# Attention's stage of a diffusion layer in the program's order on four engines, with its steps at ticks and less adaLN work inside

## The chip, the core and the metric

The kernel runs on one core of a Trainium2 chip. The metric is the device time of one execution in microseconds; three executions of the kernel before have a median of 1446.35 us (1445.36 to 1450.94). The engines are named as in the profile: PE is TensorE, DVE is VectorE, ACT is ScalarE, POOL is GpSimd and SP is the queue that issues nearly all transfers.

## The reference: what is computed

One layer of a diffusion backbone: adaLN, two-dimensional neighbourhood attention, and a gated convolutional FFN. There are 256 latent tokens (four rows of 64) and 256 context tokens, a width of 2048, 16 heads of 128 and an FFN width of 5504, all in float32. Cut to its core:

```
sh1, sc1, g1, sh2, sc2, g2 = split(silu(c) @ w_ada + b_ada, 6)
h, hc = modulate(rms_norm(x), sh1, sc1), modulate(rms_norm(ctx), csh1, csc1)
q, k, v = split(h @ w_qkv, 3); qc, kc, vc = split(hc @ w_qkv, 3)    # q and k: rms_norm per head
p = softmax(concat(q @ k_window * scale + bias, q @ kc * scale))
x = x + g1 * ((p @ concat(v, vc)) @ w_o)
hf = modulate(rms_norm(x), sh2, sc2)
x = x + g2 * conv_ffn(hf)
```

## The kernel before

**Products.** Every weight is fetched in tiles of 256 rows by 512 columns (512 KB, buffer `wr`, four of them) and split into a high and a low part: ScalarE rounds the high part `wh` (L155, three buffers), VectorE subtracts to get the low part `wl` (L156, two buffers). The activations are split in the same way (`hh` and `hl`). A product is then three matmuls: high by high, high by low, low by high. The splits are written two tiles ahead of their use (`ahead`, `weight`).

**Projections.** `project(c0, nt)` makes 512 columns (four heads, called a group) of Q, K or V for `nt` token tiles of 128: four for K and V (latent and context), two for Q (latent only). For each of eight weight tiles and each token tile it issues six matmuls of 512 columns (L378 to L380), into the PSUM banks `pj`, four in all. The order is Q0, K1, Q1, V2, K2, Q2, K3, Q3, V3 (K0, V0 and V1 come from an earlier stage). This is attention's stage; in the profile it lies between 204 and 601 us.

**Attention beside it.** While the next group is projected, the four heads of the group before are worked on: for each head two score products with bias add, maximum, exponential, sum and scaling (`scores`), two transposes of the probabilities with a high and a low part (`turn`), and the product with V (`weigh`). These pieces stand in the list `side`, from which a piece is taken after token tiles (`side.tick`), with a fractional rate. Between two groups the list is emptied, and then all K and Q tiles of the coming group are normed and transposed (`norm_transpose`): four squares with sums on ScalarE (L521), a power on GpSimd (L195), two Newton steps and a scaling on VectorE (L196 to L200, L526), four transposes on TensorE (L532), a high part on ScalarE (L534) and a low part on VectorE (L535). This is the order as written; a scheduler then sets the order of every engine's instructions, with the scores at high priority.

**adaLN beside it.** Three of adaLN's six vectors (`g1T`, `sh2T`, `gs2T`) are made in this stage too: twelve columns of 512, each the sum of eight pieces. A piece loads 512 KB (`wa`, a ring of three buffers) and multiplies it by `silu(c)`, either on ScalarE with sums on GpSimd (L276, L277) or on VectorE alone (L274, L279). A finished column is totalled (L285, on VectorE), transposed on TensorE (L288) and reduced and biased (L291, L294, L296). There are 97 pieces, placed by `ada.tick(0.44 * nt)` per weight tile, so that all are used up by the end of the stage.

**w_o.** The output projection has five groups, WO0 to WO4. WO0 covers the twelve heads that are done; beside it the rest of group 3's heads is worked on (`rest`, one piece per `cn / 340` of a tick). The others follow, with a residual step into `x1` on VectorE (L779), squares on ScalarE and their sum (L788). WO4 has 256 columns and uses the `ms` banks. Then come the norm and the FFN (products at L727 and L733).

Of the kernel before, what the change touches and what calls it, by code (L numbers as in the profile page):

```python
# [15 lines left out]
P = 128  # L16
# [10 lines left out]
KT = 2  # L27

RATE, RATE3 = 0.46, 0.36
# [21 lines left out]
def block_kernel(  # L51
# [29 lines left out]
    turns = []  # L81
# [47 lines left out]
    rp = cp.tile([NH * NDR, 31], F32, name="rp")  # L129
    nc.scalar.dma_start(rp, rpb)  # L130
# [16 lines left out]
    def wpair(src, k0, kn, c0, cn):  # L147
# [4 lines left out]
        with ExitStack() as order:  # L152
            for ins in hold:
                order.enter_context(tc.issue_after(ins))
            a = nc.scalar.copy(hi[:, :kn, :cn], w[:, :kn, :cn])  # L155
            b = nc.vector.tensor_tensor(  # L156
                out=lo[:, :kn, :cn], in0=w[:, :kn, :cn], in1=hi[:, :kn, :cn].bitcast(F32),
                op=ALU.subtract,
            )
# [7 lines left out]
    for g, cols in ((0, (0,)), (1, (D, 0)), (2, (2 * D, D, 0)), (3, (D, 0, 2 * D))):  # L167
        for c in cols:
            plan.extend((w_qkv, kt, KT, c + g * CH, CH) for kt in range(0, KD, KT))
# [21 lines left out]

    def rsqrt_newton(pool, v, n, name, bufs=2):

        r, t = [pool.tile([P, n], F32, tag=name + i, name=name + i, bufs=bufs) for i in "rt"]
        nc.gpsimd.tensor_tensor(out=r, in0=v, in1=mhalf[:, :n], op=ALU.pow)  # L195
        nc.vector.tensor_mul(t, r, r)  # L196
        nc.vector.scalar_tensor_tensor(
            out=t, in0=t, scalar=-0.5, in1=v, op0=ALU.mult, op1=ALU.mult
        )
        nc.vector.scalar_tensor_tensor(  # L200
            out=r, in0=t, scalar=1.5, in1=r, op0=ALU.add, op1=ALU.mult
        )
        return r
# [48 lines left out]
    def ada_tasks(pool, i, c, dst, gcol=None):  # L252
# [10 lines left out]
        def part(q):  # L263
# [6 lines left out]
            for k in range(KT):  # L270
                s = sT[:, q * KT + k, 0:1]
                first = q < 2 and k == 0
                if first:
                    nc.vector.tensor_scalar_mul(acc, w[:, k, :], s)  # L274
                elif pool_:
                    nc.scalar.mul(w[:, k, :], w[:, k, :], s)  # L276
                    nc.gpsimd.tensor_add(acc, acc, w[:, k, :])  # L277
                else:
                    nc.vector.scalar_tensor_tensor(  # L279
                        out=acc, in0=w[:, k, :], scalar=s, in1=acc, op0=ALU.mult, op1=ALU.add  # L280
                    )

        def finish():
            acc = st["acc", 0]
            nc.vector.tensor_add(acc, acc, st["acc", 1])  # L285
            sp = ms()
            for b in range(4):
                nc.tensor.transpose(sp[:, b * P : (b + 1) * P], acc[:, b * P : (b + 1) * P], ident)  # L288
            d = dst[:, 4 * c : 4 * c + 4]
            bc = S_B + i * KD + 4 * c  # L290
            nc.vector.tensor_reduce(  # L291
                out=d, in_=sp.rearrange("p (b t) -> p b t", t=P), axis=AX.X, op=ALU.add
            )
            nc.vector.tensor_add(d, d, sm[:, bc : bc + 4])  # L294
            if gcol is not None:
                nc.vector.scalar_tensor_tensor(  # L296
                    out=d, in0=d, scalar=1.0, in1=sm[:, gcol + 4 * c : gcol + 4 * c + 4],
                    op0=ALU.add, op1=ALU.mult,
                )

        return [(lambda q=q: load(q), lambda q=q: part(q)) for q in range(KD // KT)], finish

    def ada_pieces(cols):
# [5 lines left out]
        def piece(i):  # L309
# [5 lines left out]
            if i % n == 1 and i > n:  # L315
                cols[i // n - 1][1]()
            with tc.issue_after(last[0]), tc.issue_after(last[1]):
                if i < len(parts):
                    parts[i]()
                else:  # L320
                    cols[-1][1]()
# [15 lines left out]
    xp = xctx.enter_context(tc.tile_pool(name="xp", bufs=1))  # L337
    s32 = xp.tile([P, KD, 32], F32, name="s32")
# [31 lines left out]
    def nat(psl, tt0, w, kt0, n, first, last):  # L370

        wh, wl = w
        for i, pt in enumerate(psl):
            ts = slice((tt0 + i) * P, (tt0 + i + 1) * P)
            for k in range(n):
                kt = kt0 + k
                a, z = first and k == 0, last and k == n - 1
                nc.tensor.matmul(pt, hh[:, kt, ts], wh[:, k, :], start=a, stop=False)  # L378
                nc.tensor.matmul(pt, hh[:, kt, ts], wl[:, k, :], start=False, stop=False)  # L379
                nc.tensor.matmul(pt, hl(kt, ts), wh[:, k, :], start=False, stop=z)  # L380
# [131 lines left out]
    def row2k(name):  # L512
        return ap.tile([P, CH], F32, tag="r2", name=name, bufs=3)

    def norm_transpose(pt, gcol, dh, dl, t0):

        ss = ap.tile([P, 4], F32, tag="ss", name="ss", bufs=2)
        qn = row2k("qn")
        for h in range(4):
            hc = slice(h * HD, (h + 1) * HD)  # L520
            nc.scalar.activation(qn[:, hc], pt[:, hc], AF.Square, accum_out=ss[:, h : h + 1])  # L521
        nc.vector.tensor_scalar(
            out=ss, in0=ss, scalar1=1.0 / HD, scalar2=EPS, op0=ALU.mult, op1=ALU.add
        )
        r = rsqrt_newton(ap, ss, 4, "n")
        nc.vector.tensor_tensor(  # L526
            out=qn.rearrange("p (h d) -> p h d", d=HD), in0=pt.rearrange("p (h d) -> p h d", d=HD),
            in1=r.unsqueeze(2).to_broadcast([P, 4, HD]), op=ALU.mult,
        )
        tp = at()  # L530
        for h in range(4):
            nc.tensor.transpose(tp[:, h * P : (h + 1) * P], qn[:, h * HD : (h + 1) * HD], ident)  # L532
        tpv = tp.rearrange("p (h t) -> p h t", t=P)
        nc.scalar.activation(dh[:, :, t0 : t0 + P], tpv, AF.Copy, scale=gcol)  # L534
        nc.vector.scalar_tensor_tensor(  # L535
            out=dl[:, :, t0 : t0 + P], in0=tpv, scalar=gcol,
            in1=dh[:, :, t0 : t0 + P].bitcast(F32), op0=ALU.mult, op1=ALU.subtract,
        )
# [420 lines left out]
```

## Time and profile before

| what | value |
|---|---|
| median of three executions | 1446.35 us (1445.36 to 1450.94) |
| the profiled execution: its time, its span | 1445.85 us, 1444.0 us |
| granted clock of TensorE, mean | 0.992 |
| TensorE, VectorE, ScalarE, GpSimd busy | 97%, 69%, 54%, 19% of the span |
| attention's stage | 204 to 601 us |
| w_o, WO0 to WO4 | 601 to 702.4 us |
| boundary of the second norm | 702.4 to 717 us |

A row of a window view gives the length of a stretch, then the busy time of each engine in it with the number of its instructions, the granted clock (1.00 is full speed, and half speed is granted after idleness), the share in which the transfer engines were busy, and what they moved in GB/s. A row of a group view gives an instruction's line and engine, its output and inputs, a count, the busy time and the mean duration in ns, and then the engine's idle time ahead of it. A matmul's duration overlaps the next one's, so that a busy TensorE may still be slower than its best pace.

### The profile page before, as it was taken

What the parts mean: (1) busy time and instruction counts of PE and PEld (TensorE: products, weight loads), DVE (VectorE), ACT (ScalarE), POOL (GpSimd) and SP (SyncE); (2) the same over time, 40 slices, a digit from 0 to 9 for tenths busy, and PEclk for the clock granted to TensorE, in tenths of its full rate; (3) what the DMA queues carried; (4) which work ended last, traced back from release to release, by engine and by line L of the source; (5) the groups of instructions that cost most, each with busy time, mean ns of one, the idle gap of its engine ahead of it and who ended that gap; (6) DMA issues with size and microseconds to landing.
All of it is one profiled execution on the core that took longest, in us unless ns stands there. A gap on an engine that the chain in (4) does not pass through costs nothing.

```text
span 1444.0 us, 21091 instructions
## 1 busy us (share of the span) xinstructions
PE 1399.1 (97%) x7608; PEld 1167.8 (81%) x7608; DVE 1000.0 (69%) x1541; ACT 778.5 (54%) x1356; POOL 281.1 (19%) x208
## 2 busy tenths in 40 slices
PE   5999999999999999999899999999999999999998
PEld 2666787877787887888788888888888888888888
DVE  4556687686868768756768787887877775545454
ACT  4322265775555675755556566665666654333333
POOL 1000025465445555300101111111111000000000
PEclk9999999999999999999899999999999999999999
DMA  9999548687677677545567777777776666566554
GB/s 308 357 333 313 190 125 269 206 259 218 214 219 254 215 239 232 178 138 189 174 201 224 237 230 242 236 229 234 228 240 196 182 175 206 182 207 204 172 173 156
DMA packets 208920, 317.14 MB, mean 220 GB/s; under 512 B 23360, under 2 KB 87744, under 8 KB 208816
## 3 DMA queue, kind: packets, MB, share of 16 engines
q1 hardware_dynamic: 208688, 315.79, 70.4%
q8 instruction: 59, 0.97, 0.3%
q14 instruction: 45, 0.37, 0.1%
q10 hardware_dynamic: 128, 0.01, 0.0%
HBM read 312.75 MB, written 3.01 MB: 219 GB/s over the span
## 4 chain that ended last, share of the span: by engine, by line
PE 74%; issue 9%; DMA 5%; DVE 4%; ACT 3%; POOL 2%; SPq 1%; DVEq 0%; POOLq 0%; ACTq 0%
PE pj L727 18%; PE pj L733 9%; PE mx L727 8%; PE ms L727 7%; PE pj L379 5%; PE pj L378 5%; PE pj L380 5%; PE mx L733 4%; PE ms L733 4%; DMA wa<-in_w_ada 3%; PE ms L411 2%; PE mx L378 2%; PE mx L379 2%; PE mx L380 2%; POOL acc L277 2%
## 5 line engine op out<-in xcount | busy, mean ns | idle before, releaser
L156 DVE TENSOR_TENSOR wl<-wr,wh 128x1024 fp32r<-128x1024 f32 (+2 forms) x425 | 503.8, 1186 | 280.6 <-PE pj L733 106.3
L155 ACT CAST wh<-wr 128x1024 fp32r<-128x1024 f32 (+2 forms) x425 | 412.1, 971 | 428.8 <-PE pj L727 135.1
L277 POOL TENSOR_TENSOR acc<-acc,wa 128x512 f32<-128x512 f32 x144 | 223.6, 1553 | 428.8 <-issue 260.1
L379 PE MATMUL pj<-wl,hh 128*128 128x512 f32 x512 | 204.7, 400 | 3.5 <-DVE wl L156 3.4
L380 PE MATMUL pj<-wh,hl 128*128 128x512 f32 x512 | 201.7, 397 | 0.0
L378 PE MATMUL pj<-wh,hh 128*128 128x512 f32 x512 | 194.4, 400 | 2.5 <-ACT hh L450 2.5
L727 PE MATMUL pj<-hf,wh 128*128 128x512 f32 x688 | 176.3, 396 | 2.0 <-DVE hf L819 2.0
L727 PEld LDWEIGHTS pj<-hf,wh 128*128 128x128 f32 x688 | 124.9, 191 | 25.1 <-DVE hf L819 2.8
L276 ACT ACTIVATE wa<-wa,sT 128x512 f32<-128x512 f32 x144 | 97.4, 718 | 74.5 <-DMA wa<-in_w_ada 69.3
L379 PEld LDWEIGHTS pj<-wl,hh 128*128 128x128 f32 x512 | 97.7, 191 | 27.2 <-DVE wl L156 6.3
L378 PEld LDWEIGHTS pj<-wh,hh 128*128 128x128 f32 x512 | 96.8, 190 | 26.9 <-issue 3.4
L380 PEld LDWEIGHTS pj<-wh,hl 128*128 128x128 f32 x512 | 97.5, 191 | 19.5
L733 PEld LDWEIGHTS pj<-hf,wl 128*128 128x128 f32 x688 | 94.6, 192 | 6.8
L733 PE MATMUL pj<-hf,wl 128*128 128x256 f32 x688 | 97.8, 285 | 0.0
L727 PE MATMUL mx<-hf,wh 128*128 128x512 f32 x352 | 97.7, 394 | 0.0
L727 PE MATMUL ms<-hf,wh 128*128 128x512 f32 x336 | 90.9, 390 | 0.0
L279 DVE SCALAR_TENSOR_TENSOR acc<-wa,sT,acc 128x512 f32<-128x512 f32 x80 | 73.7, 921 | 6.9 <-DMA wa<-in_w_ada 6.3
L727 PEld LDWEIGHTS ms<-hf,wh 128*128 128x128 f32 x336 | 63.1, 188 | 14.2
L727 PEld LDWEIGHTS mx<-hf,wh 128*128 128x128 f32 x352 | 60.6, 190 | 7.8
L478 DVE TENSOR_TENSOR vsum<-vsum,mx 128x512 f32<-128x512 f32 x64 | 43.2, 684 | 34.2 <-PE mx L380 34.0
L733 PEld LDWEIGHTS mx<-hf,wl 128*128 128x128 f32 x352 | 53.7, 189 | 7.1 <-DVE wl L156 0.4
L584 POOL TENSOR_TENSOR bt<-bt,maskt 128x384 f32<-128x384 f32 x16 | 17.9, 1123 | 206.4 <-DMA bt<-rpd 173.7
(251 smaller groups left out, 2212.0 us busy)
## 6 DMA issues: line engine op xcount, KB each, us to landing
wr<-in_w_up SPq DMA_DIRECT2D x160, 512.0 KB, 4.5
wa<-in_w_ada SPq DMA_DIRECT2D x128, 512.0 KB, 4.6
wr<-in_w_qkv SPq DMA_DIRECT2D x93, 512.0 KB, 4.8
wr<-in_w_down SPq DMA_DIRECT2D x63, 512.0 KB, 4.8
wx<-in_w_ada SPq DMA_DIRECT2D x56, 512.0 KB, 8.6
wr<-in_w_o SPq DMA_DIRECT2D x24, 512.0 KB, 3.9
wr<-in_w_down SPq DMA_DIRECT2D x45, 256.0 KB, 3.0
wr<-in_w_up SPq DMA_DIRECT2D x16, 384.0 KB, 3.4
```

The costliest lines, as they stand in the source:

```text
L155: a = nc.scalar.copy(hi[:, :kn, :cn], w[:, :kn, :cn])
L156: b = nc.vector.tensor_tensor(out=lo[:, :kn, :cn], in0=w[:, :kn, :cn], in1=hi[:, :kn, :cn].bitcast(F32), op=ALU.subtract,)
L276: nc.scalar.mul(w[:, k, :], w[:, k, :], s)
L277: nc.gpsimd.tensor_add(acc, acc, w[:, k, :])
L279: nc.vector.scalar_tensor_tensor(out=acc, in0=w[:, k, :], scalar=s, in1=acc, op0=ALU.mult, op1=ALU.add)
L378: nc.tensor.matmul(pt, hh[:, kt, ts], wh[:, k, :], start=a, stop=False)
L379: nc.tensor.matmul(pt, hh[:, kt, ts], wl[:, k, :], start=False, stop=False)
L380: nc.tensor.matmul(pt, hl(kt, ts), wh[:, k, :], start=False, stop=z)
L411: nc.tensor.matmul(ap_[32 * k : 32 * k + 32, :n], s32[:, 4 * q + k, :], w[:, k * n : (k + 1) * n], start=(q == 0), stop=(q == 3), tile_pos ...
L478: nc.vector.tensor_add(acc[:, h0 + i, :], acc[:, h0 + i, :], pr_[i])
L727: nc.tensor.matmul(pts[b][:, : t1 - t0], wh[:, k, bs], mov(kt, slice(t0, t1)), start=(kt == 0 and t0 == 0), stop=False,)
L733: nc.tensor.matmul(pts[b][:, :T], wl[:, k, bs], mov(kt, slice(0, T)), start=False, stop=(kt == kn - 1),)
```

## The change

1. In attention's stage the instructions of TensorE, VectorE, ScalarE and GpSimd are kept in program order (`io`). The scheduler no longer moves them there. The transfer queue is not pinned.
2. A class `Beside` holds steps at ticks, one tick after each token tile's six products (`beside.tick()` in `nat`). Norms, transposes, scores, turns, products with V and V's split are each cut into steps one tick or more apart (`norm`, `flip`, `scores`, `turn`, `weigh`, `split_v`) and placed by numbers written out per project. The norms of K and Q stand beside the projections around them, and no longer in a block between the groups.
3. A norm has one square of a whole tile on ScalarE and a reduction on VectorE in place of four squares with sums; a power on GpSimd follows (`sums`, `scale`).
4. adaLN is thinner in the stage: 0.47 pieces per token tile, only in projects with four token tiles. 75 of the 97 pieces run in the stage; the last 22 run in w_o's groups 1 to 3, one per weight tile, and the rest of them at WO3's end. The order of the columns is `g1T`, `gs2T`, `sh2T`. Total, transpose and finish of a column are separate steps.
5. K2 is projected ahead of V2. In WO0 the list `rest` has eight pieces, one per `cn / 500`, as two scores more are done in the stage.

```diff
+    def io(ins):
+        if fixed:
+            tc.keep_in_program_order(ins)
+        return ins
...
+        def tick(self):
+            if self.on:
+                for work in self.due.pop(self.now, ()):
+                    work()
+                self.now += 1
...
-            side.tick(side.rate)
+            beside.tick()
+            ada.tick(ada.rate)
...
+        ada.rate = ADA_RATE if nt == 4 else 0.0
...
-            ada.tick(0.44 * nt)
...
+            if i > n and i % n == 1 or i == len(parts):
+                total()
+            if i > n and i % n == 3 or i == len(parts):
+                flip()
...
+        beside.put(t, squares)
+        beside.put(t + 1, sums)
+        beside.put(t + 3, scale)
...
+    norm(ks[2], t)
+    norm(qs[0], t + 1)
+    norm(ks[3], t + 3)
+    norm(qs[1], t + 4)
```

The order rows below are of VectorE, TensorE and the same places before and after. `wl` is a split's low part, `nr` and `nt` a norm's power and Newton steps, `kl` the low part of K, `qn` and `qw` a scaled tile, `acc` an adaLN column, `om` and `vv` the splits of attention's output and of V.

**VectorE in Q2.** In before, between two splits of a two-token project, stand a norm of K and its low part:

```order
L156 TENSOR_TENSOR wl_3841<-wr_3838,wh_3840 128x1024
L279 SCALAR_TENSOR_TENSOR acc_3761<-wa_3782,sT_94,acc_3761 128x512
L196 TENSOR_TENSOR nt_4003<-nr_4002 128x4
L279 SCALAR_TENSOR_TENSOR acc_3761<-wa_3782,sT_94,acc_3761 128x512
L197 SCALAR_TENSOR_TENSOR nt_4003<-nt_4003,ss_3995 128x4
L200 SCALAR_TENSOR_TENSOR nr_4002<-nt_4003,nr_4002 128x4
L526 TENSOR_TENSOR qn_3996<-oT_1589,nr_4002 128x512
L535 SCALAR_TENSOR_TENSOR kl_3931<-ms_3967,sm_69,kh_3930 128x4x128
L156 TENSOR_TENSOR wl_3863<-wr_3860,wh_3862 128x1024
L535 SCALAR_TENSOR_TENSOR kl_3931<-mx_3988,sm_69,kh_3930 128x4x128
L156 TENSOR_TENSOR wl_3887<-wr_3884,wh_3886 128x1024
```

In after, at the same project:

```order
L160 TENSOR_TENSOR wl_3744<-wr_3741,wh_3743 128x1024
L610 SCALAR_TENSOR_TENSOR kl_3711<-ms_3734,sm_69,kh_3710 128x4x128
L160 TENSOR_TENSOR wl_3772<-wr_3769,wh_3771 128x1024
L756 TENSOR_TENSOR ptl_3766<-mx_3753,pth_3765 128x4x128
L160 TENSOR_TENSOR wl_3797<-wr_3794,wh_3796 128x1024
L610 SCALAR_TENSOR_TENSOR kl_3711<-ms_3782,sm_69,kh_3710 128x4x128
L160 TENSOR_TENSOR wl_3827<-wr_3824,wh_3826 128x1024
L756 TENSOR_TENSOR ptl_3766<-mx_3806,pth_3765 128x4x128
L610 SCALAR_TENSOR_TENSOR kl_3711<-ms_3819,sm_69,kh_3710 128x4x128
L160 TENSOR_TENSOR wl_3848<-wr_3845,wh_3847 128x1024
```

The norms of K are gone from here; between two splits stand one or two steps of 512 columns, and no adaLN.

**VectorE at the end of V3 and the entry to w_o.** In before V's low parts (L559) follow adaLN's last finish, and no score of the group's last two heads stands near:

```order
L156 TENSOR_TENSOR wl_5331<-wr_5328,wh_5330 128x1024
L285 TENSOR_TENSOR acc_5136<-acc_5136,acc_5192 128x512
L294 TENSOR_TENSOR gs2T_102<-gs2T_102,sm_69 128x4
L623 RECIPROCAL rs_5171<-rs_5171 128x1
L296 SCALAR_TENSOR_TENSOR gs2T_102<-gs2T_102,sm_69 128x4
L559 TENSOR_TENSOR vv_5367<-pj_4956,vv_5367 128x512
L559 TENSOR_TENSOR vv_5367<-pj_4957,vv_5367 128x512
L559 TENSOR_TENSOR vv_5367<-pj_4958,vv_5367 128x512
L636 TENSOR_TENSOR ptl_5115<-ms_5214,pth_5114 128x4x128
L156 TENSOR_TENSOR wl_5414<-wr_5411,wh_5413 128x1024
```

In after two tops of scores (L712, L717) and two parts of `om` stand ahead of them:

```order
L160 TENSOR_TENSOR wl_5288<-wr_5285,wh_5287 128x1024
L307 TENSOR_SCALAR acc_5188<-wa_5126,sT_94 128x512
L712 TENSOR_TENSOR ms_5181<-ms_5181,bt_4965 128x256
L717 TENSOR_REDUCE nm_5199<-ms_5181 128x1
L712 TENSOR_TENSOR mx_5201<-mx_5201,bt_5085 128x256
L717 TENSOR_REDUCE nm_5215<-mx_5201 128x1
L729 RECIPROCAL rs_5212<-rs_5212 128x1
L660 TENSOR_TENSOR om_5223<-oT_1589,om_5223 128x256 x2
L649 TENSOR_TENSOR vv_5239<-pj_4659,vv_5239 128x512
L649 TENSOR_TENSOR vv_5239<-pj_4660,vv_5239 128x512
L649 TENSOR_TENSOR vv_5239<-pj_4661,vv_5239 128x512
L649 TENSOR_TENSOR vv_5239<-pj_4662,vv_5239 128x512
```

The scores that were worked on in WO0 moved to the end of V3.

**TensorE from WO3 to WO4.** In before WO4's products (bank `ms`) follow WO3's, one of them even earlier:

```order
L733 MATMUL pj_6081<-om_5376,wl_6220 128x256 x2
L733 MATMUL pj_6082<-om_5376,wl_6220 128x256 x2
L733 MATMUL mx_6083<-om_5376,wl_6220 128x256 x2
L733 MATMUL mx_6084<-om_5376,wl_6220 128x256 x2
L727 MATMUL ms_6285<-om_5376,wh_6241 128x256 x3
L727 MATMUL ms_6286<-om_5376,wh_6241 128x256 x4
```

In after the transposes of the last two adaLN columns stand between:

```order
L912 MATMUL pj_5982<-om_5223,wl_6162 128x256 x2
L912 MATMUL pj_5983<-om_5223,wl_6162 128x256 x2
L912 MATMUL mx_5984<-om_5223,wl_6162 128x256 x2
L912 MATMUL mx_5985<-om_5223,wl_6162 128x256 x2
L322 MATMUL mx_6122<-ident_71,acc_5783 128x128 x4
L322 MATMUL ms_6216<-ident_71,acc_6038 128x128 x4
L906 MATMUL ms_6247<-om_5223,wh_6189 128x256 x4
L912 MATMUL ms_6247<-om_5223,wl_6190 128x256 x2
```

The second of them reads `acc_6038`, whose total is the last row but one of what VectorE does there in after (L980 is the residual step, L989 the sum of squares, L312 an accumulation, L317 the total):

```order
L160 TENSOR_TENSOR wl<-wr,wh 128x2x256
L980 SCALAR_TENSOR_TENSOR x_5224<-pj,g1T,x_5224 128x256
L980 SCALAR_TENSOR_TENSOR x_5224<-mx,g1T,x_5224 128x256 x2
L312 SCALAR_TENSOR_TENSOR acc<-wa,sT,acc 128x512
L989 TENSOR_TENSOR sacc_5593<-sacc_5593,sq 128x256
L328 TENSOR_REDUCE sh2T<-mx 128x4
L312 SCALAR_TENSOR_TENSOR acc<-wa,sT,acc 128x512
L989 TENSOR_TENSOR sacc_5593<-sacc_5593,sq 128x256
L331 TENSOR_TENSOR sh2T<-sh2T,sm 128x4
L989 TENSOR_TENSOR sacc_5593<-sacc_5593,sq 128x256 x2
L317 TENSOR_TENSOR acc<-acc 128x512
L328 TENSOR_REDUCE sh2T<-ms 128x4
```

Ahead of the first of these rows stand five residual steps of WO3. In before no adaLN step stands here, and the splits of WO4 follow the residual steps.

More of the change, by code (lines that the diff above doesn't have):

```diff
@@ L27 @@
 KT = 2
-RATE, RATE3 = 0.46, 0.36
+ADA_RATE = 0.47
 WA = 3
@@ L512, in row2k @@
     def row2k(name):
[L513 to L538, printed above, removed]
```

488 lines of the change are left out of this document (319 added, 169 removed).

## The prediction

> **What bounds the kernel now.** I read the page first, for the engine that sets the end.
>
> ```profile
> PE 1399.1 (97%) x7608; PEld 1167.8 (81%) x7608; DVE 1000.0 (69%) x1541; ACT 778.5 (54%) x1356; POOL 281.1 (19%) x208
> ...
> PE 74%; issue 9%; DMA 5%; DVE 4%; ACT 3%; POOL 2%; SPq 1%; DVEq 0%; POOLq 0%; ACTq 0%
> ```
>
> TensorE is busy for 97% of the span and carries 74% of the chain that ended last. The change removes no product, so it can gain only what TensorE loses beside its products: idle gaps, half clock, and short waits inside runs of products, which the page counts as busy. The second view, busy time by windows, shows where that is. The windows below are attention's stage by project, cut where the project in hand changes: Q0, K1, Q1, V2, K2, Q2, K3, Q3, V3, and last the whole stage. Columns: length, busy us and matmuls of TensorE, then its weight loads, VectorE, ScalarE and GpSimd, the granted clock, the DMA share, GB/s.
>
> ```profile
> 204.00:229.00 25.00, 23.98 (x110) 19.01 (x109) 23.36 (x24) 15.25 (x21) 12.70 (x7) 1.00 0.71 224
> 229.00:285.00 56.00, 55.02 (x266) 45.22 (x265) 37.41 (x62) 35.00 (x70) 28.75 (x20) 1.00 0.72 228
> 285.00:314.50 29.50, 27.31 (x137) 22.41 (x136) 23.38 (x31) 23.27 (x56) 15.47 (x11) 1.00 0.86 273
> 314.50:375.30 60.80, 56.29 (x275) 46.04 (x274) 46.91 (x73) 32.89 (x72) 32.02 (x24) 1.00 0.70 215
> 375.30:428.60 53.30, 52.75 (x263) 44.03 (x263) 37.14 (x47) 33.58 (x68) 24.36 (x19) 1.00 0.74 224
> 428.60:459.70 31.10, 27.91 (x118) 22.10 (x117) 27.35 (x40) 19.71 (x45) 17.93 (x12) 0.89 0.77 248
> 459.70:515.00 55.30, 55.30 (x271) 45.89 (x271) 38.43 (x61) 34.46 (x69) 30.12 (x22) 1.00 0.73 227
> 515.00:543.00 28.00, 28.00 (x146) 23.60 (x145) 21.65 (x35) 20.38 (x57) 13.31 (x10) 1.00 0.79 245
> 543.00:601.00 58.00, 54.28 (x253) 43.99 (x251) 42.35 (x74) 35.53 (x73) 31.17 (x21) 0.97 0.74 227
> 204.00:601.00 397.00, 380.85 (x1826) 312.28 (x1824) 297.98 (x445) 250.08 (x522) 205.85 (x142) 0.99 0.74 231
> ```
>
> Idle in the stage is 397.00 - 380.85 = 16.2 us. Half clock adds (1 - 0.89) x 31.1 + (1 - 0.97) x 58 = 5.2 us. That is 21 us at least. A yardstick for the whole: K2 ran 263 matmuls in 53.3 us, 0.203 us each, and Q3 146 in 28.0, 0.192 each. At these paces the four-token projects K1, V2, K3 and V3 lose 2.0 + 5.0 + 0.3 + 6.6 and the two-token Q0, Q1 and Q2 3.9 + 3.2 + 8.4: 29 us. The records miss a few matmuls, so I take **27 us (21 to 29)** as what the stage can give. It sits in Q2, V2, V3, Q0 and Q1, where VectorE is busy for 73% to 93% of the window.
>
> The third view, the timeline inside Q2, shows how it is lost.
>
> ```profile
> 443.36 1.22 DVE L156 TENSOR_TENSOR wl<-wr,wh 128x1024 fp32r<-128x1024 f32 x1
> 443.53 1.92 POOL L195 TENSOR_TENSOR nr<-ss,mhalf 128x4 f32<-128x4 f32 x1 [2.70 <-DVE ss L522]
> ...
> 443.80 0.39 PE L380 MATMUL pj<-wh,hl 128*128 128x512 f32 x1
> 444.03 0.39 PE L379 MATMUL pj<-wl,hh 128*128 128x512 f32 x1
> ...
> 445.48 1.25 DVE L196 TENSOR_TENSOR nt<-nr 128x4 f32<-128x4 f32 x1 [0.25 <-POOL nr L195]
> ...
> 448.60 0.16 DVE L200 SCALAR_TENSOR_TENSOR nr<-nt,nr 128x4 f32<-128x4 f32 x1
> ...
> 450.07 1.63 DVE L156 TENSOR_TENSOR wl<-wr,wh 128x1024 fp32r<-128x1024 f32 x1
> ...
> 451.76 0.79 PE L379 MATMUL pj<-wl,hh 128*128 128x512 f32 x1 [1.50 <-DVE wl L156]
> ```
>
> Between the splits at 443.36 and 450.07 VectorE does a norm of K, and stands behind GpSimd's power. A two-token project uses a weight tile up in 12 products, 12 x 0.23 = 2.8 us (the products overlap: each lasts 0.39 us, and the one at 444.03 starts 0.23 after the one at 443.80). So 6.7 us between two splits starves TensorE, and the half clock follows.
>
> **The change, part by part.** *1. The stage's order.* The norms and transposes of K are spread over the project ahead, the splits get their place between them, and two ticks stand between a power and the Newton step that reads it. The first pair of order rows shows it at Q2: the norms of K are gone from there. Durations of the pieces that move or go:
>
> ```profile
> L156 DVE TENSOR_TENSOR wl<-wr,wh 128x1024 fp32r<-128x1024 f32 x87 | 120.3, 1384 | 28.5 <-PE pj L379 14.7 <-issue 4.2 <-ACT oT L653 2.9
> ...
> L279 DVE SCALAR_TENSOR_TENSOR acc<-wa,sT,acc 128x512 f32<-128x512 f32 x60 | 58.7, 979 | 6.8 <-DMA wa<-in_w_ada 6.3
> ...
> L274 DVE TENSOR_SCALAR acc<-wa,sT 128x512 f32<-128x512 f32 x24 | 14.2, 596 | 0.0
> ...
> L285 DVE TENSOR_TENSOR acc<-acc 128x512 f32<-128x512 f32 x12 | 8.2, 686 | 4.5 <-POOL acc L277 4.4
> ...
> L526 DVE TENSOR_TENSOR qn<-oT,nr 128x512 f32<-128x512 f32 x16 | 11.0, 688 | 0.3
> ...
> L619 DVE TENSOR_REDUCE nm<-mx 128x1 f32<-128x512 f32 x14 | 9.5, 682 | 8.5 <-ACT pr L622 8.5
> ...
> L277 POOL TENSOR_TENSOR acc<-acc,wa 128x512 f32<-128x512 f32 x108 | 166.7, 1543 | 99.5 <-ACT wa L276 53.3 <-DVE acc L274 17.7 <-ACT wh L155 13.5
> ...
> L276 ACT ACTIVATE wa<-wa,sT 128x512 f32<-128x512 f32 x108 | 73.2, 719 | 74.5 <-DMA wa<-in_w_ada 69.3 <-DVE acc L279 1.7 <-POOL acc L277 1.4
> ...
> L521 ACT ACTIVATE qn<-oT 128x128 f32<-128x128 f32 x64 | 19.0, 301 | 0.7 <-DVE nt L197 0.5
> ```
>
> ScalarE's four squares of a norm become one, which only relieves an engine that is not the bound. VectorE gains 24 sums at about 0.68 us (the price of L619's reduction of the same tile), 16.4 us, and loses the adaLN work that moves out: 14 x 0.979 + 4 x 0.596 + 3 x 0.686 + 4 x 0.68 = 20.9 us. Its load in the stage stays at some 294 us, of 375 to 390: enough, if it is spread. Added up by the new order, VectorE's work between two splits stays under TensorE's per weight tile, but for the first tile after Q1 and after Q3, where two norms of K and two of Q meet: four reductions, four scalings at 0.688, two low parts, adaLN and the small steps, some 11 us against 24 x 0.23 = 5.5 us of products and a little between them. The split two tiles ahead covers most of that. I leave 3 us for these two places and 1 us (between K3's loss of 0.3 and K1's of 2.0) for each of five project starts, where a product waits until its bank is copied out: 8 us left of 27. Bounds: 4, if the two places are covered whole, and 14, if the half clock's 5.2 us stay as well. **The stage gains 19 us (13 to 23).** The order is now pinned on four engines: what a late POOL step holds up is no longer passed by. That is in the upper bound, and in a rival.
>
> *2. The entry to w_o.* The second pair of order rows: two top steps of scores (each a bias add of 128x256, 0.42 us by L788's row below, and a maximum at 0.682) now stand ahead of V's four low parts, for which W0's first product waits. 2 x 1.1 = 2.2 us later; I take **+2** (0 to 4).
>
> *3. adaLN in w_o.* The last 22 of 97 pieces run in w_o's groups 1 to 3, which stand in two windows of before; below them are the boundary behind w_o, and what VectorE's steps cost there.
>
> ```profile
> 634.00:669.00 35.00, 34.23 (x201) 29.34 (x200) 22.29 (x35) 18.77 (x30) 0.00 (x0) 1.00 0.59 183
> 669.00:691.00 22.00, 22.00 (x128) 19.36 (x128) 13.41 (x20) 9.94 (x16) 0.00 (x0) 1.00 0.45 149
> 702.40:717.00 14.60, 8.63 (x34) 6.79 (x33) 11.18 (x24) 8.64 (x18) 3.74 (x5) 0.66 0.70 229
> ...
> L156 DVE TENSOR_TENSOR wl<-wr,wh 128x1024 fp32r<-128x1024 f32 x23 | 28.1, 1223 | 14.9 <-PE pj L733 6.4 <-PE mx L733 6.1 <-PE ms L733 1.7
> ...
> L156 DVE TENSOR_TENSOR wl<-wr,wh 128x512 fp32r<-128x512 f32 x16 | 10.9, 690 | 8.4 <-PE pj L733 3.9 <-PE mx L733 3.5 <-ACT wh L155 0.9
> ...
> L779 DVE SCALAR_TENSOR_TENSOR x<-pj,g1T,x 128x256 f32<-128x256 f32 x16 | 7.2, 479 | 3.0 <-PE pj L733 3.0
> ...
> L788 DVE TENSOR_TENSOR sacc<-sacc,sq 128x256 f32<-128x256 f32 x13 | 5.5, 421 | 0.3
> ...
> wa<-in_w_ada SPq DMA_DIRECT2D x128, 512.0 KB, 4.6
> ```
>
> There TensorE lost 0.8 us in 57, and VectorE worked 35.7. With the 20.9 us it works 56.6 of 57: full. What doesn't fit is mostly deferred to behind the products; I take **+3 us** (0 to 6).
>
> *4. WO3 to WO4.* The third pair of order rows: the last column's transposes (L322) now stand on TensorE ahead of every product of WO4, and wait for the total (L317). On VectorE stand ahead of that total, counted from the first bank that WO3 finishes, 0.7 us before its end: eight residual steps at 0.479, one split at 0.690, two accumulations at 0.979, four sums at 0.421, a reduction at 0.68, a small add at 0.16 and the total at 0.686: 9.7 us. So TensorE is idle for 9.7 - 0.7 = 9 us at least. The ring of three adaLN buffers can make it longer: from the moment the last load finds its slot it is 4.6 us to land, 2 x 0.719 on ScalarE and 2 x 1.543 on GpSimd, 9.1 us, before the total's 0.686. If that slot comes free 6 us after WO3's end, the wait is 16. I take **+11 us** (9 to 16), near the row sum, since the order puts few steps behind the slot. Nothing covers it: in before WO4's products follow at once.
>
> *5. The clock behind it.* In the boundary window an idle of 14.6 - 8.63 = 6 us goes with a clock of 0.66, which is (1 - 0.66) x 14.6 = 5 us less work. Behind an idle of 9 to 11 us I take **+2.5** (1.7 to 5). [...]
>
> Sum on the profiled execution (1445.85 us, span 1444.0): 1445.85 - 19 + 2 + 3 + 11 + 2.5 = 1445.35. That execution is 0.5 us under the median of 1446.35, so the median comes to 1445.85; rounded down, as the wait's lower end is the firmest number, **1445 us: no change**, a gain in the stage given back in w_o. 0.5% of the time, 7.2 us, is about what a measurement of this kernel can tell from no change.
>
> **The rivals.** *A, faster: the stage gives all it has.* The half clock goes (5.2 us), the two heavy tiles are covered, VectorE keeps up in w_o, and the wait is at its row sum: 1445.85 - 24 + 2 + 0 + 9 + 2 = 1435. For it: K3 and Q3 run almost without loss in before with the same work beside them. Against it: VectorE's 57 of 57 us in w_o.
>
> *B, slower: GpSimd's adds block VectorE in w_o.* Before has no GpSimd work there; after has 24 adds at 1.543 us. In Q2's timeline a step of 128x4 took 1.25 us beside GpSimd and 0.16 without: 1.1 us held. If each add holds VectorE so, 26 us come on top of 56.6 in 57, of which some 20 land on TensorE, since splits stand behind: 1445.85 - 19 + 2 + 20 + 11 + 2.5 = 1462. It decides for slower from 0.5 us an add: 12 us in place of 3, 1454. Against it: the split itself took 1384 ns in the stage, with GpSimd busy half the time, and 1223 ns in w_o without, a difference of 0.16. [...]
>
> *C, slower: the pinned order holds.* A Newton step behind GpSimd's power now also holds the splits behind it. In before the power takes 1.9 us where it stands beside an add, and two adds ahead of it make 2 x 1.543 + 1.9 = 5 us, against two ticks of 1.4 us. 24 norms, 16 of them in projects with adaLN: if 0.8 us of each reaches TensorE, 13 us of the gain go: 1445 + 13 = 1458. It decides from 0.5 us a norm. Against it: the first step of a two-token project finds GpSimd free, since adaLN is stopped there.
>
> *D: the change doesn't do what it says*, as the DMA queue is not pinned and the waits were for data. For it: ScalarE's adaLN step waited 69.3 us for its loads. Against it: where Q2 lost its time, TensorE waited for VectorE's split, and VectorE for GpSimd, not for a load. The gain would be 8, not 19: 1457.
>
> **How the numbers follow.** The forecast has 0.50, A 0.27, B 0.10, C 0.08, D 0.05. The forecast's own range is 1438 to 1453 (19 against 13 to 23, the wait's 9 to 16, and 0 to 6 for w_o, not all at one end). The range for 8 in 10 reaches to A's 1435 less 2 us for an entry that costs nothing, and to C's 1458: 1433 to 1458. Faster by over 0.5%: A whole and a few hundredths of the forecast, 0.29; slower: B, C and D, 0.23; within: 0.48.
>
> **What would show it.** In the profile of after: TensorE's idle in the stage is under 8 us and the clock there 1.00; the stage ends some 19 us sooner; in w_o's last group an idle of 9 to 12 us stands at L322 with VectorE's total as releaser, and the clock falls behind it. It is wrong if that idle is under 5 us, if TensorE waits for L160 in w_o for more than 6 us, or if the stage still loses over 14 us.

## The result and the profile after

The changed kernel takes **1487.32 us** (median of four, 1484.79 to 1489.33) against 1446.9 for the kernel before; the ratio is 1.0274, 95% interval 1.0247 to 1.0301. Forecast were 1445 us and no change, in a range of 1433 to 1458; it came out 40 us slower than the kernel before. Its profiled execution has a span of 1486.2 us and a mean clock of 0.981.

The page of after, for the same two parts as before:

```profile
PE 1406.6 (95%) x7608; PEld 1173.3 (79%) x7608; DVE 1038.5 (70%) x1565; ACT 764.1 (51%) x1190; POOL 283.9 (19%) x208
...
PE 49%; DMA 0%; DVE 0%; ACT 0%; issue 0%; POOL 0%; DVEq 0%; SPq 0%; ACTq 0%; POOLq 0%
```

TensorE lost two points of its share, and no other engine gained more than one: nothing became the bound. (The chain was followed back only to the boundary behind w_o, so it says nothing about the stage.) Where the time went is read from windows. Attention's stage is taken to the first product of w_o, and w_o to the first product of the FFN. First after, then before:

```profile
204.00:619.90 415.90, 384.97 (x1832) 316.18 (x1831) 317.99 (x474) 231.43 (x374) 170.05 (x123) 0.97 0.65 198
619.90:753.00 133.10, 109.42 (x636) 94.21 (x636) 100.52 (x147) 72.56 (x123) 40.76 (x25) 0.91 0.63 207
```

```profile
204.00:601.00 397.00, 380.85 (x1826) 312.28 (x1824) 297.98 (x445) 250.08 (x522) 205.85 (x142) 0.99 0.74 231
601.00:711.50 110.50, 103.80 (x634) 91.63 (x634) 72.37 (x129) 59.99 (x105) 0.71 (x1) 0.98 0.51 164
```

The stage up to w_o's first product is 18.9 us longer, where with the entry's 2 us it should have been 17 shorter; w_o with its boundary is 22.6 us longer. In the stage TensorE's idle time grew from 397.00 - 380.85 = 16.2 us to 415.90 - 384.97 = 30.9 us. ScalarE works less there (231 us for 250). VectorE works 20 us more, although by the prediction's sum some 5 us had left; about half of it is work that falls outside the window in before: four norms (20 there, 24 in after) and two scores.

What the engines wait for in the stage, after (engine, operation, releaser: us in total, times, longest):

```profile
ACT pr L724 <- DVE nm L717: 60.5, 17, 8.8
ACT pr L730 <- DVE rs L729: 34.8, 21, 4.9
```

```profile
DVE wl L160 <- ACT wh L159: 48.1, 28, 4.8
DVE rs L729 <- ACT pr L724: 7.7, 7, 1.5
...
DVE nt L203 <- POOL nr L198: 5.5, 8, 0.9
```

```profile
PE ms L601 <- DVE qw L585: 6.1, 3, 3.7
...
PE pj L424 <- DVE wl L160: 2.5, 4, 1.3
```

In before ScalarE's exponential waited 15.9 us for the maximum and its scaling 5.6 us for the reciprocal, and VectorE's split hardly waited for the high part. Now ScalarE waits for VectorE, and VectorE for ScalarE. TensorE itself waits only 2.5 us in all for a low part, so VectorE's 48.1 us don't reach it directly. A stretch of the timeline of after, in V2, shows one round of it:

```profile
418.83 0.69 ACT L724 ACTIVATE pr<-mx,nm 128x512 f32<-128x512 f32 x1 [5.27 <-DVE nm L717]
...
419.50 1.04 ACT L159 CAST wh<-wr 128x1024 fp32r<-128x1024 f32 x1
...
424.08 1.22 DVE L160 TENSOR_TENSOR wl<-wr,wh 128x1024 fp32r<-128x1024 f32 x1
425.21 0.16 DVE L729 RECIPROCAL rs<-rs 128x1 f32<-128x1 f32 x1
...
425.47 0.72 ACT L730 ACTIVATE pr<-pr,rs 128x512 f32<-128x512 f32 x1 [4.92 <-DVE rs L729]
...
428.20 1.04 ACT L159 CAST wh<-wr 128x1024 fp32r<-128x1024 f32 x1
...
429.27 1.68 DVE L160 TENSOR_TENSOR wl<-wr,wh 128x1024 fp32r<-128x1024 f32 x1 [2.79 <-ACT wh L159]
...
435.87 0.69 ACT L724 ACTIVATE pr<-mx,nm 128x512 f32<-128x512 f32 x1 [2.20 <-DVE nm L717]
...
437.16 1.29 DVE L649 TENSOR_TENSOR vv<-pj,vv 128x512 fp32r<-128x512 f32 x2 [1.32 <-ACT vv L646]
```

ScalarE stands 5.3 us at an exponential, makes the high part behind it, stands 4.9 us at a scaling whose reciprocal is 0.16 us of work far back in VectorE's row, and makes the next high part only behind that scaling, a copy and three adaLN multiplications. For that high part VectorE stands 2.8 us, and works without a gap from there to the next maximum at 435.15 us; the next exponential waits 2.2 us for it, and behind the exponential stand the copies of V2's banks, for which TensorE waits. The places where TensorE stands, each from the timeline of after (start, duration, and in brackets the idle ahead):

```profile
374.20 0.79 PE L423 MATMUL pj<-wh,hh 128*128 128x512 f32 x1 [3.88 <-ACT oT L805]
...
425.36 0.50 PE L424 MATMUL pj<-wl,hh 128*128 128x512 f32 x1 [1.31 <-DVE wl L160]
437.90 0.79 PE L423 MATMUL pj<-wh,hh 128*128 128x512 f32 x1 [5.86 <-DVE vv L649]
...
569.49 0.63 PE L601 MATMUL ms<-ident,qw 128*128 128x128 f32 x4 [3.69 <-DVE qw L585]
...
618.89 0.58 PE L773 MATMUL ms<-pth,vv 128*128 128x256 f32 x1 [8.86 <-DVE om L660]
...
722.39 1.08 PE L322 MATMUL mx<-ident,acc 128*128 128x128 f32 x4 [5.24 <-DVE x L980]
731.06 1.11 PE L322 MATMUL ms<-ident,acc 128*128 128x128 f32 x4 [7.58 <-DVE acc L317]
```

But for the one at 425, they lie at the seams of the stage: a bank that is not copied out (374, 437), a norm that is not done (569), the entry to w_o (618). The last two rows are the adaLN transposes ahead of WO4.

### The profile page after: what moved, and what is told of

It reads as the page before. It is cut to its first block, busy times and chain, and to the rows that moved or that the text cites. A ratio compares the mean times of both kernels' runs of the same rounds, so it can differ in the third digit from the quotient of the medians.

```text
span 1486.2 us, 20905 instructions
## 1 busy us (share of the span) xinstructions
PE 1406.6 (95%) x7608; PEld 1173.3 (79%) x7608; DVE 1038.5 (70%) x1565; ACT 764.1 (51%) x1190; POOL 283.9 (19%) x208
## 5 line engine op out<-in xcount | busy, mean ns | idle before, releaser
L160 DVE TENSOR_TENSOR wl<-wr,wh 128x1024 fp32r<-128x1024 f32 (+2 forms) x425 | 506.0, 1191 | 320.9 <-PE pj L912 99.5
L423 PE MATMUL pj<-wh,hh 128*128 128x512 f32 x512 | 207.2, 410 | 14.2 <-ACT oT L805 5.9
L309 ACT ACTIVATE wa<-wa,sT 128x512 f32<-128x512 f32 x144 | 96.5, 715 | 25.6 <-DMA wa<-in_w_ada 25.3
L312 DVE SCALAR_TENSOR_TENSOR acc<-wa,sT,acc 128x512 f32<-128x512 f32 x80 | 81.5, 1018 | 5.5 <-DMA wa<-in_w_ada 4.3
L198 POOL TENSOR_TENSOR nr<-ss,mhalf 128x4 f32<-128x4 f32 x24 | 30.9, 1288 | 136.3 <-DVE ss L577 117.9
```

Source lines behind the costliest of these rows:

```text
L160: b = io(nc.vector.tensor_tensor(out=lo[:, :kn, :cn], in0=w[:, :kn, :cn], in1=hi[:, :kn, :cn].bitcast(F32), op=ALU.subtract,))
L198: io(nc.gpsimd.tensor_tensor(out=r, in0=v, in1=mhalf[:, :n], op=ALU.pow))
L309: io(nc.scalar.mul(w[:, k, :], w[:, k, :], s))
L312: io(nc.vector.scalar_tensor_tensor(out=acc, in0=w[:, k, :], scalar=s, in1=acc, op0=ALU.mult, op1=ALU.add))
L423: io(nc.tensor.matmul(pt, hh[:, kt, ts], wh[:, k, :], start=a, stop=False))
```

## The experiments

Theories: *lock step*, that engines pinned to the written order hand their waits on to each other; *load*, that VectorE has too much to do; *adaLN in w_o*, that the stage is fine and w_o pays. Later, which of the pinned engines, and which of their steps, costs the time.

**1. No pinning.** All of after, but the scheduler sets the order again:

```diff
-        if fixed:
-            tc.keep_in_program_order(ins)
+        pass
```

> The kernel after, with its program order no longer pinned: the scheduler sets the order on all four engines, all else as after. After loses 35 us in the stage against 27 in before, about 11 us at the entry to w_o, and about 22 us in the rest of w_o. Theory 1 (lock step: pinned engines wait for each other, ScalarE's exponential for VectorE's maximum, VectorE's split for ScalarE's high part): the stage's and the entry's losses fall by 15 to 25 us, w_o's rest stays, about 1467. Theory 2 (load: VectorE has more to do, and GpSimd holds it up): the order doesn't matter, 1484 to 1490. Theory 3 (all of the loss is adaLN in w_o and the entry): 1484 to 1490 as well, but with the entry as in after.

Measured: 1458.56 us, ratio to before 1.0079 (1.0055 to 1.0102). Its profile in the stage:

```profile
204.00:591.80 387.80, 378.24 (x1834) 313.68 (x1833) 286.86 (x449) 227.17 (x367) 168.70 (x118) 0.99 0.69 212
```

The pin alone costs 28 us of the stage, more than lock step had been given; the load theory falls, since the same work runs in 388 us. TensorE's idle there is 387.80 - 378.24 = 9.6 us, against 30.9 with the pin. With the scheduler the stage is 9 us shorter than before's. The exponential's wait is 23.9 us here and VectorE's wait for high parts is gone from the list:

```profile
DVE rs L728 <- ACT pr L723: 28.7, 21, 3.8
DVE wl L159 <- PE pj L423: 17.1, 17, 2.7
```

VectorE still waits, most for the exponential's sum (28.7 us, against 7.7 in after). But its split waits for TensorE to free a buffer: there it is ahead.

**2. All of adaLN in the pinned stage** (`ADA_RATE = 0.64` for 0.47).

> The kernel after, with 0.64 adaLN pieces per tick in place of 0.47, so that all 97 are done in the stage, pinned as in after. All theories: w_o's rest loses its 22 us, the wait of 13.3 us ahead of WO4 with it. Theory 1 (lock step): 22 pieces more in the pinned stage bring waits with them, 5 to 10 us, so about 1472. Theory 2 (load): VectorE's 21 us more in the stage come back in full, 1482 to 1488. Theory 3: the stage takes them for nothing, 1465.

Measured: 1504.12 us, 1.0394 (1.0362 to 1.0425), worse than every theory said.

```profile
204.00:662.20 458.20, 398.55 (x1846) 322.43 (x1844) 345.14 (x502) 247.46 (x397) 205.69 (x147) 0.95 0.65 201
662.20:771.70 109.50, 102.24 (x620) 91.04 (x620) 69.00 (x118) 56.90 (x100) 0.71 (x1) 0.96 0.50 162
```

w_o is back at before's 110 us, but 22 pieces cost the pinned stage 458.2 - 415.9 = 42 us, some 1.9 us each.

**3. The last column's finish behind WO4's products.** In after; the last adaLN column's total, transposes and finish are moved:

```diff
         if i == len(WO) - 2:
-            ada.drain()
+            while len(ada) > 1:
+                ada.popleft()()
+        if i == len(WO) - 1:
+            ada.drain()
```

> The kernel after, with the last adaLN column's total, transposes and finish written behind WO4's products in place of ahead of them. The wait ahead of WO4 (13.3 us of idle and some 4 us of half clock behind it) goes: 1470 if it was the transposes that held the products up, and 1483 or more if the wait only moves to the norm behind WO4 or if WO4's splits are what is late. The theories on the stage say the same here.

Measured: 1475.68 us, 1.0196 (1.0171 to 1.022): 11.6 us back, between the two expectations. The last column's total and transposes were what held the products, but behind them WO4's own splits are late now:

```profile
722.59 1.21 PE L906 MATMUL ms<-om,wh 128*128 128x256 f32 x8 [1.62 <-ACT wh L159]
725.10 1.22 PE L912 MATMUL ms<-om,wl 128*128 128x256 f32 x4 [1.30 <-DVE wl L160]
```

**4. Before with after's adaLN pace.** In before, and the columns in after's order:

```diff
-            ada.tick(0.44 * nt)
+            ada.tick(0.47 * nt if nt == 4 else 0.0)
```

> The kernel before, with after's adaLN pace: 0.47 per token tile in projects with four token tiles alone, the columns in after's order, so that 22 of 97 pieces run in w_o. The order stays the scheduler's. Theory 2 (load): the stage gains 5 to 10 us from VectorE's lighter work and w_o loses 20: 1456 to 1462. Theory 1 (lock step): the stage gains little, since the scheduler passed such waits by, 0 to 5, and w_o loses 20: 1461 to 1468. If w_o's loss needs the pinned order, 1440 to 1447.

Measured: 1450.12 us, 1.0023 (1.0007 to 1.0039).

```profile
204.00:584.20 380.20, 374.48 (x1831) 310.49 (x1829) 266.30 (x421) 237.66 (x501) 162.98 (x118) 1.00 0.70 216
584.20:715.70 131.50, 108.05 (x636) 93.09 (x636) 101.61 (x154) 74.07 (x126) 43.39 (x25) 0.93 0.65 213
```

None of the expectations had the sizes: the stage gains 16.8 us, w_o with its boundary loses 21.0. The wait ahead of WO4 needs no pinned order: it is 12.4 us here. (In after, too, the pin ends ahead of WO0, at `fixed.clear()`, so w_o's own steps are in the scheduler's order in every run.)

```profile
692.76 1.09 PE L288 MATMUL ms<-ident,acc 128*128 128x128 f32 x4 [12.42 <-DVE acc L285]
```

**5. Before with after's pace and the late finish** (4 and 3 together).

> The kernel before in the scheduler's order, with adaLN at after's pace (0.47 per token tile, four-token projects alone), and the last column's total, transposes and finish written behind WO4's products. With the pace alone it took 1450, its stage 17 us shorter than before's and its w_o 21 us longer, 12.6 of these in one wait ahead of WO4. The late finish takes that wait and the half clock behind it away, as it took 11.6 us from after: 1436 to 1440, faster than before and after. If w_o's loss is VectorE's load and only moves: 1446 to 1450.

Measured: 1442.84 us, ratio 0.9958 (0.9942 to 0.9975): the lowest time but one, 0.4% under before, and 3 us above the expected range. The stage takes 382.1 us (380.2 in 4), and w_o 123.6 us; 8 of the 12 us come back.

```profile
586.10:709.70 123.60, 109.01 (x636) 93.50 (x636) 100.61 (x154) 73.87 (x126) 42.29 (x26) 0.96 0.69 228
```

**6. The same with the last three columns on ScalarE and GpSimd** (`pool_ = q % 3 != 0 or i == 3 and c > 0 and q > 0`).

> The kernel of the late finish in the scheduler's order (1443), with nearly all pieces of the last three adaLN columns on ScalarE and GpSimd: 12 steps of VectorE's fewer in w_o, 12 multiplications of ScalarE's and 12 additions of GpSimd's more. If VectorE's load is what costs that kernel 13 us in w_o: 4 to 9 us less, 1434 to 1439. If GpSimd's additions hold VectorE's steps up, as the prediction's rival B has it, or if GpSimd's chain ends late: 1443 to 1452.

Measured: 1441.54 us, 0.9957 (0.994 to 0.9975). w_o from 587.0 to 710.1 us is 123.1 us, as in 5.

```profile
587.00:710.10 123.10, 108.50 (x635) 94.06 (x635) 91.14 (x142) 80.46 (x138) 61.96 (x37) 0.96 0.69 227
```

VectorE has 9.5 us less, GpSimd 20 us more, and it changes nothing. Part of what VectorE saved in steps it lost in longer ones: its 24 large splits (L156) took 1439 ns in the mean for 1318 in 5, and its 13 sums (L791) 676 for 449, some 6 us together. This is inconclusive on why w_o is 13 us over before's: VectorE's load and GpSimd's additions were not changed one without the other. That stays open.

**7. Which engine's pin.** The condition in `io` becomes `if fixed and ins.ins.engine in (...)`. Single engines left free:

> The kernel after with TensorE, VectorE and GpSimd pinned and ScalarE left to the scheduler. All four pinned: 1487; none: 1459. In after ScalarE waits 60.5 us in the stage for VectorE's maximum and 34.8 us for its reciprocal, and VectorE 48.1 us for ScalarE's high parts. Theory 1 (lock step of ScalarE and VectorE): ScalarE can pass its exponential by and do the high part, VectorE's wait for it falls under 15 us, and half or more of the 28 us comes back: 1462 to 1473. Rival (the steps' ticks are too tight on VectorE alone): 1480 to 1487. Rival C of the prediction (GpSimd's power): 1480 to 1487.

> The kernel after with TensorE, ScalarE and GpSimd pinned and VectorE left to the scheduler. Theory 1 (lock step): half or more of the 28 us comes back here as well, since a ring of waits opens at any of its links: 1462 to 1473. Rival (VectorE alone is too tight): nearly all comes back here and little with ScalarE left free: 1459 to 1464. Rival C (GpSimd's power): 1480 to 1487.

> The kernel after with GpSimd left to the scheduler and the other three pinned. Rival C of the prediction (a power behind adaLN's adds holds VectorE's Newton step, and with it the splits): 10 us or more come back, 1465 to 1477. Theory 1 (lock step of ScalarE and VectorE): VectorE waited for the power only 5.5 us in after's stage, so 1483 to 1488.

> The kernel after with TensorE left to the scheduler and ScalarE, VectorE and GpSimd pinned. If TensorE's own pin is a cost by itself: the stage falls to 396 to 406, 1468 to 1477. If TensorE only waits for what the other three bring late (lock step, theory 1): the stage stays at 411 to 417, 1482 to 1488.

And more of them:

> The kernel after with TensorE alone pinned. The stage takes 416 us with all four pinned, 404 with ScalarE free, 417 with VectorE free, 411 with GpSimd free, 388 with none pinned. If TensorE's own pin is the rest of the cost (a transpose or a score that is not ready holds the products behind it): the stage stays at 398 to 406, 1468 to 1476. If the other three pins together are the cost (lock step, theory 1): the stage is 388 to 393, 1458 to 1464.

> The kernel after with TensorE and ScalarE left to the scheduler, VectorE and GpSimd pinned. If the costs of ScalarE's and TensorE's pins add up: the stage is 388 to 395, 1459 to 1466. If ScalarE's pin is the only one of the two that costs: 402 to 406 as with ScalarE free alone, 1473 to 1479.

> The kernel after with TensorE and GpSimd pinned, ScalarE and VectorE left to the scheduler. The stage took 404 us with ScalarE free, 390 with TensorE alone pinned. Theory 1 (lock step of ScalarE and VectorE, GpSimd a bystander): 388 to 393, 1458 to 1464. If GpSimd's pinned order (a power with adaLN's adds queued behind it) is the rest: 400 to 404, 1471 to 1477.

> The kernel after with TensorE and VectorE pinned, ScalarE and GpSimd left to the scheduler. Theory 1 (lock step of ScalarE and VectorE): VectorE's own pin stays, 400 to 404, 1471 to 1477. If GpSimd's pinned order is the rest of the cost: 389 to 394, 1459 to 1465.

> The kernel after with TensorE and ScalarE pinned, VectorE and GpSimd left to the scheduler. If ScalarE's pinned order is enough for the lock step (its exponential waits for the maximum, the high parts behind it): 404 to 412, 1475 to 1483. If a lock step needs two pinned engines: 388 to 396, 1458 to 1467.

| pinned | median us | ratio to before (interval) | stage us |
|---|---|---|---|
| all four (after) | 1487.32 | 1.0274 (1.0247 to 1.0301) | 415.9 |
| PE, ACT, POOL (VectorE free) | 1489.45 | 1.0282 (1.026 to 1.0304) | 416.9 |
| ACT, DVE, POOL (TensorE free) | 1487.47 | 1.027 (1.0242 to 1.0298) | 416.2 |
| PE, ACT (VectorE, GpSimd free) | 1486.24 | 1.0261 (1.024 to 1.0284) | 414.7 |
| PE, ACT, DVE (GpSimd free) | 1482.77 | 1.0244 (1.0214 to 1.0274) | 411.1 |
| PE, DVE, POOL (ScalarE free) | 1476.78 | 1.0199 (1.0172 to 1.0226) | 404.2 |
| PE, POOL (ScalarE, VectorE free) | 1474.55 | 1.0178 (1.0157 to 1.0199) | 404.9 |
| DVE, POOL (TensorE, ScalarE free) | 1470.97 | 1.0158 (1.0132 to 1.0185) | 402.7 |
| PE, DVE (ScalarE, GpSimd free) | 1468.79 | 1.0137 (1.0111 to 1.0162) | 396.2 |
| PE | 1461.23 | 1.0086 (1.0059 to 1.0113) | 390.3 |
| none (1) | 1458.56 | 1.0079 (1.0055 to 1.0102) | 387.8 |

With TensorE pinned in each, ScalarE's pin alone costs the stage 414.7 - 390.3 = 24.4 us, GpSimd's 14.6 and VectorE's 5.9; together 25.6. The costs overlap: ScalarE's written order is enough for nearly all of it, and freeing VectorE or TensorE alone gives nothing. Each stage time is of one profiled execution; the medians give the same differences within 2 us. Lock step in its strict form, that it takes ScalarE and VectorE pinned together and that freeing either of them opens it, falls: 1462 to 1473 us were expected with one of the two free, 1477 came with ScalarE free and 1489 with VectorE free, and the row of PE and ACT is as slow as all four. What stands is that the waits of a pinned ScalarE, whichever order VectorE has, delay what is written behind them. With PE and ACT alone pinned ScalarE waits longer for the maximum than in after, and VectorE still waits for high parts:

```profile
ACT pr L724 <- DVE nm L717: 79.1, 20, 6.5
```

```profile
DVE wl L160 <- ACT wh L159: 33.0, 27, 4.5
```

**8. Which steps.** The weights' splits alone left free, on ScalarE and VectorE (each pinned step stays behind the pinned step ahead of it), then adaLN's steps alone, on all four engines:

> The kernel after, pinned on four engines as before but for the weights' splits (high part on ScalarE, low part on VectorE), which the scheduler may move among the pinned steps. If splits behind waiting steps are the cost (VectorE waited 48 us for high parts): the stage falls from 416 to 392 to 402, 1463 to 1474. If the waits among attention's and adaLN's steps are: 410 to 417, 1481 to 1488.

> The kernel after, pinned on four engines but for adaLN's steps, which the scheduler may move. If adaLN's steps in a fixed place are the cost (22 pieces more cost the pinned stage 42 us, and the scheduler's order 17): the stage falls to 392 to 402, 1463 to 1474. If not: 410 to 417, 1481 to 1488.

Measured: 1478.92 us, 1.0218 (1.0201 to 1.0235), and 1481.3 us (its four executions from 1476 to 1487), 1.0219 (1.0194 to 1.0245); the stages take 410.0 and 411.2 us. With the splits free VectorE's wait for high parts is gone:

```profile
DVE wl L160 <- PE pj L424: 20.1, 19, 4.3
DVE ptl L756 <- ACT pth L753: 17.0, 15, 3.7
DVE rs L729 <- ACT pr L724: 11.9, 12, 1.5
```

and yet of its 48 us only 6 come back in the stage: other waits of VectorE, for `pth` and `rs`, stand in their place, and TensorE, which had waited little for splits, still waits at the seams:

```profile
PE ms L601 <- DVE qw L585: 9.0, 3, 4.9
PE pj L423 <- DVE vv L649: 6.7, 1, 6.7
```

Last, more distance between the steps of a score:

```diff
-for d, work in ((0, product), (1, top), (2, exp), (3, scale)):
+for d, work in ((0, product), (1, top), (3, exp), (5, scale)):
```

> The kernel after, pinned, with a score's exponential three ticks behind its product and the scaling five, in place of two and three. ScalarE waited 60 us for the maximum and 35 for the reciprocal in after. If the ticks are only too tight there: the stage falls to 398 to 408, 1468 to 1479. If the pinned order makes up a wait wherever a step is late: 411 to 418, 1482 to 1490.

Measured: 1490.54 us, 1.0298 (1.0281 to 1.0315), stage 417.3 us. The exponential's wait falls by 28 us, and the scaling's grows by 21:

```profile
ACT pr L730 <- DVE rs L729: 56.1, 20, 7.5
ACT pr L724 <- DVE nm L717: 32.3, 12, 5.6
```

So neither the splits nor adaLN's steps are most of the cost by themselves, and more ticks between maximum, exponential and scaling don't help.

## Why the prediction was wrong

*What bounds the kernel.* The account of before's losses held: with the thinner adaLN in the scheduler's order (experiment 4) the stage ran at 380 us, 17 us under before, of 27 that were said to be there.

*1. The stage's order, a gain of 19 us (13 to 23).* This is the step that failed. To w_o's first product the stage is 18.9 us longer where 17 less were forecast, 36 us off; some 6 of that belong to the entry (2), some 30 to this step. It read "Added up by the new order, VectorE's work between two splits stays under TensorE's per weight tile", and left 8 us of loss: 3 us at two heavy places and 1 us for each of five project starts. The part on splits held: TensorE waited 2.5 us in all for a low part. The term that failed is what was left for the seams. There TensorE waited 5.9 us for ScalarE's copies out of banks, 5.9 us for V's split and 7.3 us for the scaled tiles of norms, besides the entry. The sign set for it was an idle of under 8 us at full clock; it was 30.9 us at 0.97.

The sum that led there is a sum of durations on one engine. It has no place for the time in which an engine stands at a step whose input another engine makes late, while all that is written behind waits too. ScalarE appears in it only as "an engine that is not the bound": with 231 us of work in 416 it isn't, and with TensorE pinned its written order alone cost 24 us. The 18.9 us add up from three runs. Fewer adaLN pieces gain 16.8 us (4), which the prediction put down to the order. The other new steps cost 387.8 - 380.2 = 7.6 us in the scheduler's order (1 against 4; two scores more stand in that stage). The pin costs 28.1 us (after against 1).

*2. The entry, +2 (0 to 4).* The idle there is 8.86 us, against 0.81 us at w_o's first product in before, and w_o's products run at half clock (0.50 granted from 619.9 to 625.1 us), (1 - 0.50) x 5.2 = 2.6 us more. The prediction counted VectorE's two tops alone. They ran without idle ahead of them; but the first exponential waited for its maximum, and VectorE then stood for the high part of `om`, which stands on ScalarE behind two exponentials, two adaLN multiplications and a scaling:

```profile
614.48 0.69 ACT L724 ACTIVATE pr<-ms,nm 128x512 f32<-128x512 f32 x1 [3.86 <-DVE nm L717]
...
618.08 1.15 DVE L660 TENSOR_TENSOR om<-oT,om 128x256 fp32r<-128x256 f32 x2 [2.50 <-ACT om L659]
```

Without the pin (1) the idle at that place, ahead of the first product with V, is 4.4 us.

*3. adaLN in w_o, +3 (0 to 6).* In size right: between 660 and 717 us TensorE was idle for 57 - 51.8 = 5.2 us, against 0.8 us in the two windows of before.

```profile
660.00:717.00 57.00, 51.78 (x288) 42.67 (x286) 54.85 (x69) 34.36 (x52) 27.35 (x16) 1.00 0.87 286
```

*4. WO3 to WO4, +11 (9 to 16).* Right in place, mechanism and size: 5.24 + 7.58 = 12.8 us at L322, the first released by WO3's residual steps, the second by the total. Experiment 3 shows that the last column's finish is the cause, as 11.6 us go with it; experiment 4 that before has the same wait with after's adaLN pace.

*5. The clock behind it, +2.5 (1.7 to 5).* In size right. Half clock lasted from 720.7 to 734.3 us (0.50 granted), but it costs only where TensorE works, 4.33 us of these 13.6: 1.1 us at the first transposes and 3.24 us behind the second wait, (1 - 0.50) x 4.3 = 2.2 us. No run shows the range's lower end of 1.7 us; what the runs showed in its place are these 2.2 us. (The prediction's 5 us for the boundary counted idle time as well.)

```profile
722.39:723.47 1.08, 1.08 (x4) 0.68 (x4) 1.08 (x3) 1.08 (x4) 1.00 (x2) 0.50 0.21 72
731.06:734.30 3.24, 3.24 (x15) 3.24 (x16) 0.85 (x2) 0.00 (x0) 0.00 (x0) 0.50 0.00 0
```

*Rival A* fell with step 1. *Rival B* (GpSimd's adds block VectorE in w_o) was right that they slow it, and put the price at twice what came: 26 us on VectorE against some 13 (last section), of which TensorE shows the 4.4 us more of idle under 3. *Rival C* (the pinned order holds) had the right class at a chance of 0.08, with the wrong carrier and half the price: VectorE waited 5.5 us for GpSimd's power, less than before's 8.3, and with GpSimd free only 4.5 us came back; its pin costs 14.6 us where ScalarE is free, though, which after's own trace doesn't show. *Rival D* fell: the pin sets the order and changes the time by 28 us, and ScalarE's waits for adaLN's loads in the stage fell from 69.3 to 12.4 us while the stage grew.

What stays open: how ScalarE's 24 us divide among its steps. As single changes the splits' places account for some 6 us and adaLN's for some 5, and both runs freed steps of other engines too; the copies out of PSUM (the 3.88 us at 374) and the exponentials weren't freed alone.

## What to carry to other kernels

Before an order is fixed by hand, add up not only each engine's work but follow one item around the engines: in a fixed order each late input is handed on to everything written behind it, on an engine that is half idle as well (here ScalarE, with 231 us of work in 416). Fixing one engine can cost nearly as much as fixing all (here 24.4 us of 25.6, beside a pinned TensorE), and freeing one nothing (a stage of 416.2 us with TensorE free and 416.9 with VectorE free, for 415.9), so such costs are measured against the free order and not one at a time from the fixed one. Work that a later product doesn't need, such as an adaLN column's transposes, belongs behind that product in the order (here 11.6 us).

## What the runs showed of the hardware

VectorE's split (L160), accumulation (L312) and sum of squares (L989) were longer in the mean beside GpSimd's additions. In after, from 660 to 723 us (busy 31 us on GpSimd):

```profile
L160 DVE TENSOR_TENSOR wl<-wr,wh 128x1024 fp32r<-128x1024 f32 x16 | 23.7, 1487 | 0.0
L312 DVE SCALAR_TENSOR_TENSOR acc<-wa,sT,acc 128x512 f32<-128x512 f32 x13 | 16.2, 1246 | 1.9 <-DMA wa<-in_w_ada 1.9
...
L989 DVE TENSOR_TENSOR sacc<-sacc,sq 128x256 f32<-128x256 f32 x9 | 5.9, 657 | 0.0
```

Sorted by whether an instruction of GpSimd's runs at the same time, the means of this window are, without and with: split 1213 and 1840 ns (with, from 1209 to 2321), accumulation 741 and 1531, sum 412 and 853; the residual step L980, which reads a PSUM bank, took 471 ns both ways. One such meeting, a sum of squares begun beside three additions:

```profile
680.34 5.03 POOL L310 TENSOR_TENSOR acc<-acc,wa 128x512 f32<-128x512 f32 x3 [5.94 <-DVE acc L307]
...
684.14 1.52 DVE L989 TENSOR_TENSOR sacc<-sacc,sq 128x256 f32<-128x256 f32 x1
```

Over 38 steps that is some 13 us. The transfers, busier here than in before's w_o (a share of 0.87 against 0.45 to 0.59), are not the cause: steps with no addition beside them keep the times of before's w_o (1213 ns for 1223 at the split, 412 for 421 at the sum). What in an addition makes them longer is not shown: the residual step, of which one input is a PSUM bank, kept its time, but one multiplication of a single tile (L307) that met the additions took 0.92 us for 0.47 too. The prediction's doubt, drawn from an average of 0.16 us, took the stage's mean for the price of a meeting: in before's stage, too, the split took 1221 ns without GpSimd beside it and 1550 with.
